# Slots of a routed expert: one plain transfer per expert on SyncE instead of one indirect gather per block on GpSimd, and token gathers one block further ahead

## The chip, the core and the metric

The kernel runs on one core of a Trainium2 chip. The metric is device time in microseconds (us) of one execution. A core has TensorE (PE; its weight loads are PEld), VectorE (DVE), ScalarE (ACT), GpSimd (POOL) and SyncE (SP), each with an instruction queue of its own that is worked off in order, and 16 DMA engines that all queues share. SP issues plain transfers; POOL issues the indirect ones, whose row numbers lie in on-chip memory.

## What is computed

One decoder layer for 1024 tokens of width 1024. The first two thirds (attention and a recurrent mixer) are not touched here. The last third is a mixture of experts: every token is routed to 6 of 64 experts, each a SwiGLU of inner width 256, and a shared expert sees all tokens.

```python
dest = pad_start[sorted_e] + arange(n_assign) - grp_start[sorted_e]   # a slot for each (token, choice)
row_tok[dest], row_w[dest] = token, weight
...
y = swiglu(h[tok], w_gate[e], w_up[e], w_down[e]) * w[:, None]        # per block of slots
out = segment_sum(ys, row_tok)  + swiglu(h, sw_gate, sw_up, sw_down)
```

All arithmetic is float32, done as three products of a high and a low part (`three`), so each expert's weights (three arrays of 1 MB) are split into high and low on ACT and DVE before TensorE can use them.

## The kernel before

**The slot table.** In DRAM, `d_slot` holds 64 x 1152 rows of two words, (token number, weight). While tokens are routed, POOL scatters 48 batches of such rows into it (`route`, line 1676). `ranks` then sorts the experts by how many tokens they got: `eid` (line 1772) holds the expert number of each rank, and `sidx` (line 1779) for each rank and block the table rows of its 128 slots.

**Blocks.** `BLOCKS` gives each rank one to four blocks of at most 128 slots: 84 blocks for 64 experts. `order` mixes experts with several blocks among those with one. In `experts`, blocks 0 to 7 are the shared expert's (their tokens are plain loads), blocks 8 to 91 the routed ones.

**One routed block** needs, in this order: its slots (`slots`, line 1932, an indirect gather of 8 bytes a row by POOL into tile `sl`); its token rows (`rows`, line 1940, an indirect gather by POOL of up to 128 rows of 4 KB into one of four tiles `xg`, with the token numbers in `sl`); a transposition on TensorE (`turn`, lines 1952 and 1965, `tp<-idf,xg`); gate and up products; an activation; the down product; a scaling by weight and gate on DVE (`result`, line 2026, `ye`, three tiles); and an indirect scatter by POOL that adds `ye` onto the rows of `d_acc` in DRAM (line 2028). Scatters add to the same tensor, so each waits until the one before it has landed.

**Order of issue.** In iteration b of the loop in `experts`, the instructions of several blocks are interleaved: the gate/up products of block b, `need_x(b + 3)` (token rows of block b+3), `need_s(b + 5)` (slots of block b+5), the transposition of block b+1, the down product and `result` of block b-1 with its scatter. So POOL's queue reads: scatter of b-2, token rows of b+3, slots of b+5, scatter of b-1, and so on. The first slots, of blocks 8 to 12, are fetched in `dispatch`, and `experts` waits for its mark ("slots", 0) at b = 6, where it asks for the token rows of blocks 8 and 9.

**Weights.** SP issues the three 1 MB loads of an expert (`fetch`, line 1884) after it has read the expert's number out of `eid` into a register (`values_load`). `need_w(k + 4)`, once per expert, brings gate and up of expert k+4 and down of expert k+3; each has three buffers, so SP waits there until the split of an earlier expert is done. In `dispatch`, before the first slots, `need_w` runs for experts 1 to 3: eight loads.

The whole program is interleaved by a planner from the costs that the functions yield (`[("POOL", 1.0)]` and the like); it sets the order in each queue, not when an instruction runs.

Of the kernel before, what the change touches and what calls it, by code (L numbers as in the profile page):

```python
# [8 lines left out]
F32 = mybir.dt.float32  # L9
# [28 lines left out]
class Kern:  # L38
# [1699 lines left out]
    def ranks(self, pg):  # L1738

        nc, i64, t = self.nc, self.i64, self.dt  # L1740
        ps = lambda: pg.tile([128, 512], F32, name="g")
        G = ("alloc", ("g", 2)), ("free", "g")
        cr = ps()
        for j in range(8):
            nc.tensor.matmul(cr[:, 0:NE], self.onesb, self.Mb[:, j, :], start=(j == 0), stop=(j == 7))
        crow = t("crow", [128, NE])
        nc.vector.tensor_copy(crow, cr[:, 0:NE])
        yield [G[0], ("PE", .4), ("DVE", .12), G[1]]
        cc = ps()
        for j in range(8):  # L1750
            nc.tensor.matmul(cc[0:NE, 0:1], self.Mb[:, j, :], self.onesb[:, 0:1], start=(j == 0), stop=(j == 7))
        pk = self.pk = t("pk", [NE, 2])
        nc.vector.tensor_copy(pk[:, 1:2], cc[0:NE, 0:1])
        nc.vector.tensor_copy(pk[:, 0:1], self.tok[0:NE, 0:1])
        yield [G[0], ("PE", .4), ("DVE", .14), G[1]]
        lt = t("lt", [NE, NE])
        nc.vector.tensor_scalar(lt, i64[0:NE], pk[:, 0:1], None, op0=OP.is_lt)
        a = t("a", [NE, NE])
        nc.vector.scalar_tensor_tensor(a, crow[0:NE], pk[:, 1:2], lt, op0=OP.is_equal, op1=OP.mult)
        nc.vector.scalar_tensor_tensor(a, crow[0:NE], pk[:, 1:2], a, op0=OP.is_gt, op1=OP.add)  # L1760
        yield [("DVE*", .45)]
        rank = t("rank", [NE, 1])
        nc.vector.tensor_reduce(rank, a, op=OP.add, axis=AX.X)
        perm = self.perm = t("perm", [NE, NE])
        nc.vector.tensor_scalar(perm, i64[0:NE], rank, None, op0=OP.is_equal)

        eb = t("eb", [NE, 128])
        nc.vector.tensor_copy(eb, pk[:, 0:1].to_broadcast([NE, 128]))
        yield [("DVE*", .4)]
        po = ps()  # L1770
        nc.tensor.matmul(po[:, 0:NE], eb, perm, start=True, stop=True)
        self.eid = t("eid", [1, NE], I32)
        nc.vector.tensor_copy(self.eid, po[0:1, 0:NE])

        self.sidx = []
        for j in range(4):
            n = max(r + 1 for r in range(NE) if len(self.BLOCKS[r]) > j)
            x = t(f"sidx{j}", [128, n], I32)
            nc.vector.tensor_scalar(x, po[:, 0:n], float(SLOTS), self.tok[:, j:j + 1], op0=OP.mult, op1=OP.add)
            self.sidx.append(x)  # L1780
        yield [G[0], ("PE", .2), ("DVE", .5), G[1]]

    def leftover(self, pg):

# [58 lines left out]
    def phase_b(self, pg, close_a4, h2):  # L1843
# [84 lines left out]
            yield [("set", ("shared w", 0))]  # L1928

        def slots(idx, n):  # L1930
            sl = B["fp"].tile([128, 2], F32, name="sl", bufs=8)
            nc.gpsimd.indirect_dma_start(out=sl[0:n], out_offset=None, in_=self.d_slot, in_offset=ind(idx[0:n]))  # L1932
            return sl

        def tokens(sl, n):
            return sl.bitcast(I32)[0:n, 0:1]

        def rows(ti, n):
            x = B["fp"].tile([128, D], F32, name="xg", bufs=4)
            nc.gpsimd.indirect_dma_start(out=x[0:n], out_offset=None, in_=self.d_h2, in_offset=ind(ti), bounds_check=T - 1,  # L1940
                                         oob_is_err=False)
            return x
# [104 lines left out]
                if 0 < kk < NK:  # L2047
                    to[kk] = fetch(self.eid[0:1, order[kk]:order[kk] + 1], which)

        def need_s(b):  # L2050
            if b < NB:
                k, j, n = blocks[b]
                r = order[k]
                sls[b] = slots(self.sidx[j][:, r:r + 1], n) if r >= 0 else None

        def need_t(b):
            if b < NB:
                tis[b] = tokens(sls[b], blocks[b][2]) if sls[b] else self.toki[:, b:b + 1]

        def need_x(b):  # L2060
            if b < NB:
                k, j, n = blocks[b]
                if k == 0:
                    x = xs[b] = B["fp"].tile([128, D], F32, name="xg", bufs=4)
                    nc.sync.dma_start(x, self.d_ht[j])
                else:
                    xs[b] = rows(tis[b], n)

        def weight_of(b):
# [7 lines left out]
        def dispatch():  # L2077
            yield [("wait", ("route", 7))]
            expert_pools()
            yield from self.ranks(pg)  # L2080
            for k in range(1, 4):
                need_w(k)
            yield from self.leftover(pg)
            yield [("wait", ("block pools", 0))]
            for b in range(8, 13):
                need_s(b)
                yield [("POOL", 1.0)]
            yield [("DMA", 4.0)]
            yield [("set", ("slots", 0))]

        def experts():

            yield [("wait", ("block pools", 0))]
            yield [("wait", ("shared w", 0))]
            for b in range(8):
                i = blocks[b][1]
                sls[b], tis[b] = None, self.toki[:, i:i + 1]
            xs[0] = h2[6]
            for b in (1, 2):
                need_x(b)  # L2100
            G = ("alloc", ("g", 2)), ("free", "g")
            xt = turn(xs[0], 128)
            yield [("PE", .9), ("ACT", 1.0), ("~DVE", 1.2)]
            act = None
            for b in range(NB + 1):
                if b < NB:
                    k, j, n = blocks[b]
                    m = max(n, MIN_M)
                    two = xt[1] is None
                    for s in up(xt, sets[k % 2], m):  # L2110
                        if b < 8:
                            yield s
                    z = B["z"]
                    if b < 5:
                        yield [("wait", ("T", blocks[b + 3][1]))]
                        need_x(b + 3)
                    elif b == 6:
                        yield [("wait", ("slots", 0))]
                        for i in range(8, 12):
                            need_t(i)  # L2120
                        need_x(8)
                        need_x(9)
                    elif b > 6:
                        need_x(b + 3)
                    if b > 7:
                        need_s(b + 5)
                    turnover = k + 1 < NK + 1 and (blocks[b - 1][0] != k if k else b == 6)
                    if turnover and k + 1 < NK:
                        work.append(split_gu(raws[k + 1], k + 1))
                    pieces(3)  # L2130
                    if turnover and b < 8:
                        yield [("~ACT", 1.7), ("~DVE*", 1.8)]
                if b < NB and two:
                    low(z)
                if act is not None:
                    at = act_t(*act)
                    if b < 8:
                        yield [G[0], ("PE", .25), ("ACT", .3), ("DVE", .35), G[1]]
                if b + 1 < NB:
                    xt = turn(xs[b + 1], blocks[b + 1][2], b < 7)  # L2140
                    if b < 8:
                        yield [("~ACT", 1.0), ("~DVE*", 1.2)]
                if b < NB and two:
                    join(z)
                if act is not None:
                    for s in down(at, act[1]):
                        if b < 8:
                            yield s
                    zs = B["zs"]
                if b < NB:  # L2150
                    act = swiglu(z, m), m
                    pieces(99)
                    if b < 8:
                        yield [("~ACT", .6), ("~DVE", .35)]
                if b > 0:
                    result(zs, blocks[b - 1][2], weight_of(b - 1), tis[b - 1])
                    if b < 8:
                        yield [("~DVE", 1.35), ("~POOL", 1.0)]
                if b < NB:
                    if k and blocks[b - 1][0] != k:  # L2160
                        work.append(split_d(rawd[k]))
                        pieces(99)
                    if b > 7:
                        need_t(b + 4)
                    if turnover:
                        need_w(k + 4)
                    if turnover and b < 8:
                        yield [("~ACT", 2.0), ("~DVE", 2.3), ("~POOL", 1.0)]
# [93 lines left out]
```

## Time and profile before

| | us |
|---|---|
| median of 3 runs | 2097.12 |
| lowest, highest | 2080.12, 2115.2 |
| the profiled execution | 2093.02 |
| its span, first to last instruction | 2091.1 |

All durations below come from the profiled execution. In its span PE is busy 1858.6 us (89%), DVE 1470.3 (70%), ACT 933.1 (45%), POOL 859.6 (41%); the mean granted TensorE clock is 0.918. The routed experts run from about 1200 us to 2060 us. In a row of the profile, `out<-in` names the tiles by the program's names, `x8` counts merged instructions, a time in square brackets is how long the engine was idle before the instruction, with what ended the idle time ("issue": nothing that the profile shows).

### The profile page before, as it was taken

The page shows a single profiled execution, that of the slowest core. Times are in us where ns is not written, and L with a number is a line of the kernel's source. Part 1 is how long each engine was busy: PE and PEld are TensorE (multiplying, and loading weights), DVE is VectorE, ACT ScalarE, POOL GpSimd, SP SyncE. Part 2 cuts the span into 40 slices and gives each one's busy share as a digit, 9 for nine tenths or more (in the row PEclk, how much of TensorE's full clock was granted, in tenths as well). Part 3 has the DMA queues.
Part 4 walks back from the last instruction along what each step waited for, and adds up shares of the span by engine and source line. Part 5 has one row for each costly group of instructions (what it writes and reads, how often), then busy time and mean ns, then how long its engine had stood idle before and what let it go on. Part 6 is the DMA issues. An engine that isn't in the chain of part 4 may idle for free. (4 is left out here: it accounts for less than half of the span.)

```text
span 2091.1 us, 28436 instructions
## 1 busy us (share of the span) xinstructions
PE 1858.6 (89%) x9729; PEld 1399.2 (67%) x9729; DVE 1470.3 (70%) x2561; ACT 933.1 (45%) x1431; POOL 859.6 (41%) x660
## 2 busy tenths in 40 slices
PE   3999999969997997997999799989988989989993
PEld 3777677747876664654787687767756767766771
DVE  7736867939457555656677758878767878878894
ACT  5443433312322332344323236556545656666673
POOL 1201110100012232335455634765656767766662
PEclk7999789969987888998999899999989999999997
DMA  7125345462756648964664589989889999988874
GB/s 270 36 81 126 88 111 129 131 156 71 216 148 183 190 123 237 133 195 137 229 211 147 159 277 322 314 256 318 293 261 309 304 305 307 326 297 297 307 242 174
DMA packets 268579, 440.03 MB, mean 210 GB/s; under 512 B 127445, under 2 KB 197161, under 8 KB 242450
## 3 DMA queue, kind: packets, MB, share of 16 engines
q1 hardware_dynamic: 210978, 365.47, 54.0%
q0 software_dynamic: 26176, 58.91, 12.4%
q10 hardware_dynamic: 31280, 13.83, 2.5%
q8 instruction: 78, 1.28, 0.3%
q14 instruction: 67, 0.55, 0.1%
HBM read 355.27 MB, written 94.90 MB: 215 GB/s over the span
## 5 line engine op out<-in xcount | busy, mean ns | idle before, releaser
L2028 POOL DMA_INDIRECT d_acc<-ye,sl x84 | 192.1, 2287 | 253.4 <-issue 56.2
L1932 POOL DMA_INDIRECT sl<-d_slot,d_sidx x84 | 201.6, 2400 | 27.5 <-issue 24.7
L1904 ACT ACTIVATE wdh<-down 128x1024 fp32r<-128x1024 f32 x128 | 128.7, 1053 | 82.2 <-PE yd L1976 82.2
L1898 DVE TENSOR_TENSOR gul<-up,guh 128x1024 fp32r<-128x1024 f32 x128 | 155.5, 1215 | 10.4 <-ACT guh L1897 9.7
L1940 POOL DMA_INDIRECT xg<-d_h,sl x84 | 149.0, 1774 | 25.6 <-issue 20.7
L1898 DVE TENSOR_TENSOR gul<-gate,guh 128x1024 fp32r<-128x1024 f32 x128 | 155.2, 1213 | 1.7 <-ACT guh L1897 1.7
L1905 DVE TENSOR_TENSOR wdl<-down,wdh 128x1024 fp32r<-128x1024 f32 x128 | 150.1, 1210 | 0.8
L2026 DVE SCALAR_TENSOR_TENSOR ye<-yd,sl,g 128x512 f32<-128x512 f32 (+12 forms) x168 | 120.2, 740 | 32.0 <-PE yd L1976 32.0
L1897 ACT ACTIVATE guh<-gate 128x1024 fp32r<-128x1024 f32 x128 | 134.1, 1047 | 18.8 <-DMA gate<-in_exp_w_gate_dram 18.8
L1976 PE MATMUL yd<-wdh,ah 128*128 128x512 f32 (+6 forms) x368 | 130.5, 438 | 8.5 <-ACT ah L2012 6.7
L1897 ACT ACTIVATE guh<-up 128x1024 fp32r<-128x1024 f32 x128 | 135.1, 1055 | 1.5 <-DMA up<-in_exp_w_up_dram 1.5
L450 PE MATMUL zp<-hTh,whi 128*128 128x512 f32 x480 | 132.4, 414 | 1.4 <-ACT whi L373 1.4
L450 PE MATMUL zp<-hTl,whi 128*128 128x512 f32 x480 | 132.1, 412 | 0.0
L450 PE MATMUL zp<-hTh,wlo 128*128 128x512 f32 x480 | 131.9, 413 | 0.0
L1976 PE MATMUL gu<-guh,xh 128*128 128x512 f32 (+6 forms) x504 | 127.3, 394 | 0.8 <-ACT xh L1959 0.5
L1976 PE MATMUL gu<-guh,xl 128*128 128x512 f32 (+6 forms) x504 | 127.4, 395 | 0.1
L1976 PE MATMUL yd<-wdh,al 128*128 128x512 f32 (+6 forms) x368 | 123.4, 418 | 4.2 <-DVE al L2014 3.7
L1976 PE MATMUL gu<-gul,xh 128*128 128x512 f32 (+6 forms) x504 | 127.0, 394 | 0.0
L1976 PE MATMUL yd<-wdl,ah 128*128 128x512 f32 (+6 forms) x368 | 122.3, 415 | 0.3 <-DVE wdl L1905 0.3
L2012 ACT ACTIVATE ah<-g 128x256 fp32r<-128x256 f32 (+5 forms) x92 | 31.2, 339 | 179.0 <-PE g L2010 178.3
L450 PEld LDWEIGHTS zp<-hTh,whi 128*128 128x128 f32 x480 | 92.6, 198 | 26.4 <-issue 5.5
L1976 PEld LDWEIGHTS gu<-guh,xh 128*128 128x128 f32 (+6 forms) x504 | 89.1, 177 | 29.1 <-ACT xh L1959 1.0
(477 smaller groups left out, 4238.9 us busy)
## 6 DMA issues: line engine op xcount, KB each, us to landing
gate<-in_exp_w_gate_dram SPq DMA_DIRECT2D x64, 1024.0 KB
up<-in_exp_w_up_dram SPq DMA_DIRECT2D x64, 1024.0 KB
down<-in_exp_w_down_dram SPq DMA_DIRECT2D x64, 1024.0 KB
mw<-in_ada_w_dram SPq DMA_DIRECT2D x32, 512.0 KB
wraw<-in_w_in_dram SPq DMA_DIRECT2D x30, 512.0 KB
xw<-in_ada_w_dram SPq DMA_DIRECT2D x8, 1024.0 KB
xw<-in_x_dram SPq DMA_DIRECT2D x8, 512.0 KB
fb<-d_fb SPq DMA_DIRECT2D x16, 256.0 KB
```

The lines of the kernel that those rows point to most:

```text
L450: nc.tensor.matmul(z, a[:, d, :], b[:, d, hs], start=(n == 0 and d == 0), stop=(n == 2 and d == 7))
L1897: nc.scalar.activation(gh[:, qs, n, :], t[:, qs], AF.Copy)
L1898: nc.vector.tensor_sub(gl[:, qs, n, :], t[:, qs], gh[:, qs, n, :].bitcast(F32))
L1904: nc.scalar.activation(dh[:, j], raw[0][:, j], AF.Copy)
L1905: nc.vector.tensor_sub(dl[:, j], raw[0][:, j], dh[:, j].bitcast(F32))
L1932: nc.gpsimd.indirect_dma_start(out=sl[0:n], out_offset=None, in_=self.d_slot, in_offset=ind(idx[0:n]))
L1940: nc.gpsimd.indirect_dma_start(out=x[0:n], out_offset=None, in_=self.d_h2, in_offset=ind(ti), bounds_check=T - 1, oob_is_err=False)
L1976: nc.tensor.matmul(z, x[:, d, :], w[:, d, cs], start=(m == 0), stop=(m == 3 * n - 1))
L2012: nc.scalar.activation(ah[:, :, 0:n], tp[:, :, 0:n], AF.Copy)
L2026: nc.vector.scalar_tensor_tensor(y[0:n, hs], zs[h][0:n], wt, B["g2"][0:n, hs], op0=OP.mult, op1=OP.mult)
L2028: nc.gpsimd.indirect_dma_start(out=self.d_acc, out_offset=ind(ti), in_=y[0:n], in_offset=None, bounds_check=T - 1, oob_is_err=False, compu ...
```

## The change

Slots are no longer gathered per block by POOL. `need_s(k)` works per expert: SP reads the expert's number once more and issues one plain transfer of the expert's first 128, 256, 384 or 512 table rows into a tile `sk` (nine buffers), from which each block takes its two columns. It is called for experts 1 to 5 in `dispatch`, after the eight weight loads, and then for expert k+6 just ahead of `need_w(k + 4)`. `sidx` goes. Token rows are asked for as `need_x(b + 4)` in place of `need_x(b + 3)`; at b = 6 for blocks 8 and 9 as before, at b = 7 for blocks 10 and 11. The number of `xg` tiles stays at four.

```diff
@@ ranks
-        self.sidx = []
-        for j in range(4):
-            ...
-            nc.vector.tensor_scalar(x, po[:, 0:n], float(SLOTS), self.tok[:, j:j + 1], op0=OP.mult, op1=OP.add)
@@ phase_b
-        def need_s(b):
-            if b < NB:
-                k, j, n = blocks[b]
-                r = order[k]
-                sls[b] = slots(self.sidx[j][:, r:r + 1], n) if r >= 0 else None
+        table = self.d_slot.rearrange("(e r) w -> e r w", e=NE)
+        def need_s(k):
+            if 0 < k < NK:
+                r, nb = order[k], len(self.BLOCKS[order[k]])
+                e = nc.values_load(self.eid[0:1, r:r + 1], engines=(SP,), min_val=0, max_val=NE - 1)
+                sl = B["fp"].tile([128, 4, 2], F32, name="sk", bufs=9)
+                nc.sync.dma_start(sl[:, 0:nb], table[ds(e, 1)].rearrange("e r w -> (e r) w").rearrange(
+                    "(j p) w -> p j w", p=128)[:, 0:nb])
+                for b in range(NB):
+                    if blocks[b][0] == k:
+                        sls[b] = sl[:, blocks[b][1]]
@@ dispatch
-            for b in range(8, 13):
-                need_s(b)
-                yield [("POOL", 1.0)]
+            for k in range(1, 6):
+                need_s(k)
@@ experts
                     elif b == 6:
                         yield [("wait", ("slots", 0))]
-                        for i in range(8, 12):
-                            need_t(i)
-                        need_x(8)
-                        need_x(9)
+                        for i in range(8, 10):
+                            need_x(i)
                     elif b > 6:
-                        need_x(b + 3)
-                    if b > 7:
-                        need_s(b + 5)
+                        if b == 7:
+                            need_x(10)
+                        need_x(b + 4)
...
                     if turnover:
+                        need_s(k + 6)
                         need_w(k + 4)
```

## Rows read from the trace of the kernel before

**Rows 1.** Windows: start:end length, busy us (instructions) of PE, PEld, DVE, ACT, POOL; clock, DMA share, GB/s.
```profile
1200.00:2060.00 860.00, 802.25 (x3715) 610.02 (x3713) 687.96 (x892) 508.72 (x748) 539.90 (x248) 0.96 0.88 289
1500.00:1550.00 50.00, 40.09 (x178) 30.34 (x177) 32.48 (x43) 24.11 (x36) 29.61 (x14) 0.86 0.83 254
1550.00:1600.00 50.00, 50.00 (x239) 36.97 (x238) 45.19 (x58) 34.06 (x48) 35.05 (x13) 1.00 0.98 326
```

**Rows 2.** Token tiles: who waited until what (us, times), 1200 to 2080 us.
```profile
  DMA xg<-d_h,sl: 45.5, 13
...
DMA to landing us min/median/max: 4.3/10.0/14.4
```

**Rows 3.** Timeline of TensorE: transpositions of blocks 8 and 9, and a late one.
```profile
1206.05 1.06 PE L1965 MATMUL tp<-idf,xg 128*128 128x128 f32 x8
...
1215.60 1.06 PE L1965 MATMUL tp<-idf,xg 128*128 128x128 f32 x8
...
1531.45 1.68 PE L1965 MATMUL tp<-idf,xg 108*128 108x108 f32 x8 [9.84 <-DMA xg<-d_h,sl]
```

**Rows 4.** Timeline of POOL and of DVE around the longest wait.
```profile
1509.52 7.16 POOL L2028 DMA_INDIRECT d_acc<-ye,sl  x1 [2.15 <-DVE ye L2026]
1516.98 1.52 POOL L1940 DMA_INDIRECT xg<-d_h,sl  x1 [0.30 <-issue]
...
1528.19 1.60 POOL L2028 DMA_INDIRECT d_acc<-ye,sl  x1 [6.24 <-issue]
...
1517.46 1.40 DVE L2026 SCALAR_TENSOR_TENSOR ye<-yd,sl,g 108x512 f32<-108x512 f32 x2
```

**Rows 5.** Line 2028 (scatters): durations ns, first and last start; landing; 1195 to 2080.
```profile
L2028 POOL DMA_INDIRECT d_acc<-ye,sl x84: 1362/1608/7284, 1236.7 to 2059.3; - x84
L2028 POOL DMA_INDIRECT d_acc<-ye,toki x3: 1597/1614/1917, 1201.6 to 1225.0; - x3
...
DMA to landing us min/median/max: 4.0/8.8/17.8
```

**Rows 6.** Timeline of POOL: scatters held by POOL's queue, first and last of 18.
```profile
1324.05 1.43 POOL L2028 DMA_INDIRECT d_acc<-ye,sl  x1 [0.31 <-DVE xl L1968]
...
2020.54 1.40 POOL L2028 DMA_INDIRECT d_acc<-ye,sl  x1 [0.30 <-issue]
```

**Rows 7.** Line 1932 (slot gathers): durations ns min/median/max, first and last start.
```profile
L1932 POOL DMA_INDIRECT sl<-d_slot,d_sidx x84: 877/1003/6658, 1186.8 to 2018.5; - x84
```

**Rows 8.** Page, part 5: busy us, mean ns of one, idle before.
```profile
L2028 POOL DMA_INDIRECT d_acc<-ye,sl x84 | 192.1, 2287 | 253.4 <-issue 56.2
L1932 POOL DMA_INDIRECT sl<-d_slot,d_sidx x84 | 201.6, 2400 | 27.5 <-issue 24.7
```

**Rows 9.** Timeline of POOL and DVE: a long slot gather beside subtractions.
```profile
1489.69 6.65 POOL L1932 DMA_INDIRECT sl<-d_slot,d_sidx  x1 [0.31 <-issue]
...
1489.71 2.34 DVE L1905 TENSOR_TENSOR wdl<-down,wdh 128x1024 fp32r<-128x1024 f32 x2
...
1494.25 1.21 DVE L1898 TENSOR_TENSOR gul<-gate,guh 128x1024 fp32r<-128x1024 f32 x1
```

**Rows 10.** Timeline of SP: first and last of the first eight weight loads.
```profile
1184.28 0.37 SPq L1884 DMA_DIRECT2D gate<-in_exp_w_gate_dram  x1
...
1190.63 0.34 SPq L1884 DMA_DIRECT2D down<-in_exp_w_down_dram  x1
```

**Rows 11.** Timeline of POOL: the first gather of token rows.
```profile
1193.64 1.02 POOL L1940 DMA_INDIRECT xg<-d_h,sl  x1 [0.30 <-DMA sl<-d_slot,d_sidx]
```

**Rows 12.** Timeline of ACT: first uses of the first two weight loads.
```profile
1190.20 1.06 ACT L1897 ACTIVATE guh<-gate 128x1024 fp32r<-128x1024 f32 x1 [18.80 <-DMA gate<-in_exp_w_gate_dram]
1192.76 1.06 ACT L1897 ACTIVATE guh<-up 128x1024 fp32r<-128x1024 f32 x1 [1.51 <-DMA up<-in_exp_w_up_dram]
```

**Rows 13.** DMA queue of small packets: packets, MB, share of 16 engines; from the page.
```profile
q10 hardware_dynamic: 31280, 13.83, 2.5%
```

**Rows 14.** Waits of SP's queue, 1200 to 2080 us: total us, times, longest.
```profile
SPq L1884 <- DVE gul L1898: 388.1, 76, 27.7
```

More of the change, by code (lines that the diff above doesn't have):

```diff
@@ L1773, in ranks @@
         nc.vector.tensor_copy(self.eid, po[0:1, 0:NE])
-        self.sidx = []
-        for j in range(4):
-            n = max(r + 1 for r in range(NE) if len(self.BLOCKS[r]) > j)
-            x = t(f"sidx{j}", [128, n], I32)
-            nc.vector.tensor_scalar(x, po[:, 0:n], float(SLOTS), self.tok[:, j:j + 1], op0=OP.mult, op1=OP.add)
-            self.sidx.append(x)
-        yield [G[0], ("PE", .2), ("DVE", .5), G[1]]
+        yield [G[0], ("PE", .2), ("DVE", .1), G[1]]
     def leftover(self, pg):
@@ L1930, in slots @@
         def slots(idx, n):
-            sl = B["fp"].tile([128, 2], F32, name="sl", bufs=8)
+            sl = B["fp"].tile([128, 2], F32, name="sl", bufs=2)
             nc.gpsimd.indirect_dma_start(out=sl[0:n], out_offset=None, in_=self.d_slot, in_offset=ind(idx[0:n]))
@@ L2048, in need_w @@
                     to[kk] = fetch(self.eid[0:1, order[kk]:order[kk] + 1], which)
-        def need_s(b):
-            if b < NB:
-                k, j, n = blocks[b]
-                r = order[k]
-                sls[b] = slots(self.sidx[j][:, r:r + 1], n) if r >= 0 else None
+        table = self.d_slot.rearrange("(e r) w -> e r w", e=NE)
[9 more added lines that the diff above has]
+                        sls[b] = sl[:, blocks[b][1]]
         def need_t(b):
             if b < NB:
-                tis[b] = tokens(sls[b], blocks[b][2]) if sls[b] else self.toki[:, b:b + 1]
+                tis[b] = tokens(sls[b], blocks[b][2])
         def need_x(b):
@@ L2066, in need_x @@
                 else:
+                    need_t(b)
                     xs[b] = rows(tis[b], n)
@@ L2162, in experts @@
                         pieces(99)
-                    if b > 7:
-                        need_t(b + 4)
                     if turnover:
+                        need_s(k + 6)
                         need_w(k + 4)
```

## The prediction, made before the changed kernel was run

> **What bounds the kernel now.** I read the windows first. In the stage of the routed experts, 1200 to 2060 us, TensorE is busy 802 of 860 us [rows 1]; in 1550 to 1600 it has no gap at all, in 1500 to 1550 it idles 9.91 us and its granted clock falls to 0.86. So TensorE sets the pace and has holes. The token tiles name the holes: transpositions waited 13 times, 45.5 us in all, until a gather of token rows landed [rows 2]; the longest wait is 9.84 us [rows 3].
>
> A hole also costs clock. The window with the long wait holds 178 matmuls, the one after it 239: 61 fewer, at 50/239 = 0.209 us each 12.8 us of work lost for 9.91 us idle. At that ratio the 45.5 us cost 45.5 x 12.8/9.91 = 59 us. That is the most that earlier token rows can give.
>
> Why are the rows late? I followed one case through POOL's queue. The gather that TensorE waited for at 1531 was issued at 1516.98, behind a scatter that began at 1509.52 and lasted 7.16 us [rows 4]. The scatter after it began at 1528.19, although its `ye` had been ready since 1517.46 + 1.40 = 1518.86, and although POOL had been idle for 6.24 us before it. What it waited for was the landing of the scatter before: scatters go one at a time. 87 of them begin between 1201.6 and 2059.3 [rows 5], one per 857.7/86 = 9.97 us, and the median time to landing is 8.8 us of that. TensorE on its own would need (857.7 - 59)/86 = 9.29 us per block; a full block takes it 1215.60 - 1206.05 = 9.55 [rows 3]. **So POOL's chain of scatters is about as slow as TensorE**, and token rows, which stand behind a scatter in the same queue, are late whenever this chain has fallen a block behind.
>
> **The change, part by part.**
>
> *One block more of lead.* `need_x(b + 4)` stands where `need_x(b + 3)` stood, behind the same scatter, and is needed one block later: 9.55 us more. The tile it overwrites is that of block b, transposed an iteration earlier, so four tiles suffice. If the scatters were fast and only now and then late, this would cover nearly each wait (longest 9.84). But their chain runs at 9.97 per block with 9.29 wanted, so its lag grows until TensorE waits again; the lead delays this once. Gain: one block, 9.5 us; bounds 0 (lag refilled at once) and 59 (rival A).
>
> *84 slot gathers leave POOL.* 201.6 us of POOL's time, 2.40 us mean and 1.00 median [rows 7, 8]. Most lies in the wait for a landing and costs nothing. It counts where a scatter began directly, about 0.30 us, behind other work of POOL: 18 of them [rows 6]. Each begins at best one ordinary gather earlier, 1.00 + 0.30 = 1.3 us: 18 x 1.3 = 23 us at most. Half of it I expect to reach TensorE, which doesn't wait in every stretch: 11.5 us.
>
> Why only 1.3 us, where many slot gathers last 6.6? One began at 1489.69 and ended at 1496.34, 0.9 us after DVE's run of subtractions of the weights' low parts, 1489.71 to 1495.46 [rows 9]: POOL stood still while they ran. Without this gather the next instruction of POOL that falls into such a run stands still instead. The Trainium skill (SBUF — State Buffer, section "SBUF: two separate sides") says that DVE with two inputs in SBUF holds a port pair that GpSimd's operations need, and that the loser blocks fully; the trace agrees, with 6.65 us against the 1.00 median. By that rule a transfer issued by SyncE escapes the block, but not the gathers and scatters that stay on POOL.
>
> *The first slots move behind the first weights.* This part costs. Slots of block 8 were gathered by POOL at once, and its token rows were asked for at 1193.64 [rows 11]; TensorE transposed them at 1206.05. Now the slots of experts 1 to 5 are SP's next transfers after eight loads of 1 MB issued from 1184.28 to 1190.63 [rows 10]. That queue hands over one load after the other: the first two, the head of these eight, were first used at 1190.20 and 1192.76 by ACT, which had waited for each [rows 12], so 2.56 us per MB. The eighth lands at 1190.20 + 7 x 2.56 = 1208.1 at the earliest, and at 1190.20 + 7 x 3.63 = 1215.6 at the stage's mean of 289 GB/s [rows 1]. Fewer gathers compete early on, so I take 1209.5. The token rows follow 0.3 us later, and land 4.3 to 14.4, median 10.0, us after issue [rows 2]: at 1219.8. TensorE stops for 1219.8 - 1206.05 = 14 us; with 2 us of lowered clock behind it (2.9 behind the 9.91 above), 16 us, that nothing hides, since block 8 is TensorE's next work. Bounds: 1208.1 + 0.3 + 4.3 gives 6.6; 1215.6 + 0.3 + 10.0 gives 19.9, with clock 22.8. Zero, if small transfers overtake the loads.
>
> The Trainium skill (DMA: Bandwidth & Descriptors, "Queues, rings and completion order") says that an SP queue's descriptors are consumed in ring order, while different queues take turns. By that rule the slots wait for all eight loads, whereas POOL's queue took turns with them. [rows 12] agree as far as equal loads go; a small transfer behind a large one isn't in these rows.
>
> *Later slots.* Per expert SP reads one register more and issues one transfer more. Eight loads with their register reads took 1190.63 - 1184.28 = 6.35 us [rows 10], so about 0.8 us per expert of 13.4 us. SP spends 388 us waiting for DVE's splits [rows 14], and weights have three buffers: nothing. If that cover were gone, 63 x 0.8 = 50 us. Slots of expert k+6 leave two experts, 27 us, before the token rows need them; three loads of 3.63 us ahead of them make 11. SP might wait for a free `sk` tile, but nine are more than the blocks in flight.
>
> *DMA.* 84 x 128 = 10752 rows of 8 bytes replace 7616 (the block sizes' sum). The queue of small packets prices one at 2.5% of 16 engines' 2091 us over 31280 [rows 13], 27 ns: 3136 more cost 3136 x 0.027/16 = 5 us of each engine, in a stage with a share of 0.88 [rows 1]. I take 0 and keep 5 for the top of the range. The four small DVE operations of `sidx` leave: below 0.5 us together by their width against [rows 9].
>
> **Sum**: -9.5 - 11.5 + 16 = -5, from the profiled execution's 2093.0 (span 2091.1 and 1.9 around it; 4.1 below the median of 2097.1): **2088 us**. This case's own range: 2093 - 9.5 - 23 + 6.6 = 2067 to 2093 + 22.8 + 5 = 2121.
>
> **Rivals.** *A, all waits go.* The waits were single late gathers, and one block of lead (9.55) covers each. 2093 - 59 + 16 = 2050, without the stop at the start 2034. For it: no wait is longer than 9.84, and the gather's median landing is 10.0. Against: scatters at 9.97 per block, which no extra lead makes faster. Chance 0.17.
>
> *B, slower: the block by DVE moves onto the scatters.* Slot gathers absorbed 84 x (2.40 - 1.00) = 118 us of standing still. If scatters, each of which delays the next, now take half, that is 59 us in the chain: 2093 - 5 + 59 = 2147. It decides once a scatter's mean duration goes from 2.29 us [rows 8] beyond about 2.29 + 47/84 = 2.85, which makes +42. Against: a scatter that now begins inside a run of subtractions mostly stood behind a slot gather held by the same run. Chance 0.08.
>
> *C, the start costs nothing*, small transfers overtake the loads: 2093 - 21 = 2072, inside my range and its chance.
>
> **How the numbers follow.** The forecast with C has 0.75, A 0.17, B 0.08. 2% of the median is 42 us, about what a measurement of this kernel, whose runs spread over 35 us, can tell from no change: faster means below 2055, slower above 2139. So A is faster, B slower, the rest within. The range 2046 to 2122 holds this case and A with its stop; A without it and B lie outside.
>
> **What would show it.** Right: a wait of 7 to 20 us ahead of TensorE's first routed transposition; later waits for token rows fewer, but not gone (15 to 35 us in all); scatters still spaced about 9.6 to 9.9 us with a median landing near 8.8. Wrong: no waits left after the start (A), a scatter's mean duration near 3 us (B), a first token gather issued before 1200 us after a start like today's (C).

## The result, and the profile after

The change made the kernel slower. The median of four runs is 2161.7 us (2150.12 to 2164.13) against 2098.43 for the kernel before on the same chip (four runs): ratio 1.0306, 95% interval 1.026 to 1.0352. The forecast of 2088 us and its range to 2122 are both below it. All ratios and intervals compare fast executions of the two kernels on the same chip (now and then one is slower), so a ratio can differ by some tenths of a per cent from the quotient of the medians. The profiled execution of the changed kernel took 2164.13 us, span 2162.3, mean granted clock 0.904 (before 0.918).

Of the 71 us between the two spans, 50 lie between the start of block 8's scatter and that of block 91's (822.5 us before, 872.7 after). 14 lie in the new stop at the start. What is left, some 7 us, was there before the routed experts began (the scatter of block 0 starts at 1140.7 in place of 1132.3). Over all the kernels below that start lies between 1127 and 1141, and block 0 comes before anything that the change moves, so I don't count it to the change; where it comes from no run tells.

**The start** is as forecast in place and size. The timeline of the changed kernel, SP, POOL and TensorE (start us, duration us, instruction, idle time before it and what ended it):

```profile
1199.10 0.34 SPq L1877 DMA_DIRECT2D down<-in_exp_w_down_dram  x1
1200.28 13.92 SPq L2051 DMA_DIRECT2D sk<-d_slot  x6
...
1218.75 1.06 POOL L1933 DMA_INDIRECT xg<-d_h,sk  x1 [25.54 <-DMA sk<-d_slot]
...
1228.03 1.33 PE L1958 MATMUL tp<-idf,xg 128*128 128x128 f32 x5 [14.39 <-DMA xg<-d_h,sk]
```

The first slot transfer leaves SP at 1200.28, behind the eighth load (1199.10). POOL gets the slots at 1218.75, 18.5 us later. TensorE stands still for 14.39 us; I had 14. The first token gather had been issued at 1193.64 before [rows 11]. The same slot transfer ahead of the loads is of use after 2.9 us at most (experiment 4), so what it waits for here are the megabytes ahead of it in its queue. That agrees with the ring order of which the Trainium skill tells (DMA: Bandwidth & Descriptors, "Queues, rings and completion order").

**SP** now waits for something that wasn't in the forecast. Waits of SP's queue after, 1200 to 2130 us (total us, times, longest):

```profile
SPq L2051 <- DMA d_acc<-ye,sk: 416.6, 52, 20.7
SPq L1877 <- DVE gul L1891: 126.0, 29, 26.1
```

Before, SP was held by the splits on DVE, 388.1 us [rows 14]. That wait has shrunk to 126.0, and in its place SP waits 52 times, 416.6 us, at the slot transfer, until a scatter has landed.

**POOL, DVE and TensorE**: part 5 of the page after (busy us, mean ns of one, idle us before it with its releaser), the row of `ye` from the page before, then the waits of TensorE after, 1200 to 2150:

```profile
L2021 POOL DMA_INDIRECT d_acc<-ye,sk x84 | 233.3, 2777 | 452.1 <-DVE ye L2019 173.0
L2019 DVE SCALAR_TENSOR_TENSOR ye<-yd,sk,g 128x512 f32<-128x512 f32 (+12 forms) x168 | 119.5, 741 | 138.2 <-issue 61.9
L1933 POOL DMA_INDIRECT xg<-d_h,sk x84 | 179.4, 2135 | 50.9 <-DMA sk<-d_slot 25.5
L1969 PEld LDWEIGHTS yd<-wdh,al 128*128 128x128 f32 (+6 forms) x368 | 63.0, 183 | 94.6 <-DVE al L2007 74.7
```

```profile
L2026 DVE SCALAR_TENSOR_TENSOR ye<-yd,sl,g 128x512 f32<-128x512 f32 (+12 forms) x168 | 120.2, 740 | 32.0 <-PE yd L1976 32.0
```

```profile
PE yd L1969 <- DVE al L2007: 51.5, 32, 3.2
PE tp L1958 <- DMA xg<-d_h,sk: 24.9, 10, 14.4
PE tp L1945 <- DMA xg<-d_h,sk: 11.7, 6, 3.2
```

The scatter's own duration rose from 2287 ns [rows 8] to 2777. Waits for token rows beyond the start fell by half: 24.9 + 11.7 less the 14.4 of the start are 22.2 us, against 45.5 [rows 2]. But DVE idles 138.2 us ahead of `ye` (32.0 before), and TensorE has a wait that it hardly had: 51.5 us (3.7 before) for `al`, the low part of the activations, which DVE makes.

**How these hang together** shows in one stretch after, SP, DVE, POOL and TensorE:

```profile
1548.70 0.35 SPq L2051 DMA_DIRECT2D sk<-d_slot  x1
1549.90 0.34 SPq L1877 DMA_DIRECT2D gate<-in_exp_w_gate_dram  x1
1550.48 0.33 SPq L1877 DMA_DIRECT2D up<-in_exp_w_up_dram  x1
1551.63 0.34 SPq L1877 DMA_DIRECT2D down<-in_exp_w_down_dram  x1
1561.64 0.34 SPq L2051 DMA_DIRECT2D sk<-d_slot  x1
...
1548.77 1.41 DVE L2019 SCALAR_TENSOR_TENSOR ye<-yd,sk,g 128x512 f32<-128x512 f32 x2 [9.20 <-issue]
1550.09 1.22 DVE L1891 TENSOR_TENSOR gul<-gate,guh 128x1024 fp32r<-128x1024 f32 x1
...
1553.49 0.30 DVE L2007 TENSOR_TENSOR al<-g,ah 128x144 fp32r<-128x144 f32 x1
...
1561.62 1.40 DVE L2019 SCALAR_TENSOR_TENSOR ye<-yd,sk,g 56x512 f32<-56x512 f32 x2 [5.44 <-DMA d_acc<-ye,sk]
...
1549.55 1.61 POOL L2021 DMA_INDIRECT d_acc<-ye,sk  x1 [8.86 <-DVE ye L2019]
1551.47 1.86 POOL L1933 DMA_INDIRECT xg<-d_h,sk  x1 [0.30 <-issue]
1562.39 2.08 POOL L2021 DMA_INDIRECT d_acc<-ye,sk  x1 [9.06 <-DVE ye L2019]
...
1553.85 1.13 PE L1969 MATMUL yd<-wdh,al 128*72 128x512 f32 x2 [1.64 <-DVE al L2007]
```

At 1561.62 a landing lets DVE write the next `ye`; at 1561.64 SP's slot transfer goes out, at 1562.39 the next scatter starts. 1548.70, 1548.77 and 1549.55 are the same three steps one block earlier (the profile names no releaser for that `ye`, but the scatter before had landed at 1548.69). All three engines wait for the same scatter. What SP and DVE then start falls on the next one. SP sends the slots and an expert's three megabytes within 2.93 us (1548.70 to 1551.63), just as the scatter starts; it lands 10.4 us after its end, against 6.71 on average. DVE, having made `ye`, runs its overdue subtractions beside the scatter and the gather behind it. This scatter still took 1.61 us only; others, as at 1521.70 with 7.79 us, last until such a run is over. `al` comes behind the subtractions at 1553.49, and TensorE stops for it.

Before, such loads went out one by one, most of them behind a split. SP's timeline before:

```profile
1505.27 0.34 SPq L1884 DMA_DIRECT2D gate<-in_exp_w_gate_dram  x1
1508.22 0.33 SPq L1884 DMA_DIRECT2D up<-in_exp_w_up_dram  x1
1511.81 0.34 SPq L1884 DMA_DIRECT2D down<-in_exp_w_down_dram  x1
1515.21 0.34 SPq L1884 DMA_DIRECT2D gate<-in_exp_w_gate_dram  x1
```

No weights came too late for it: ACT waited for `gate` and `up` once each in the whole execution after, 18.9 and 1.4 us, much as at the start before [rows 12]. If SP's wait costs time, it is by when the loads run.

### The profile page after: what moved, and what is told of

Its sections match the earlier page's. It is cut to its first block, busy times and chain, and to the rows that moved or that the text cites. A ratio compares the mean times of both kernels' runs of the same rounds, so it can differ in the third digit from the quotient of the medians.

```text
span 2162.3 us, 28802 instructions
## 1 busy us (share of the span) xinstructions
PE 1887.6 (87%) x9729; PEld 1412.5 (65%) x9729; DVE 1464.9 (68%) x2557; ACT 932.1 (43%) x1431; POOL 732.1 (34%) x576
## 3 DMA queue, kind: packets, MB, share of 16 engines
q8 instruction: 78, 1.28, 0.2%
## 5 line engine op out<-in xcount | busy, mean ns | idle before, releaser
L2021 POOL DMA_INDIRECT d_acc<-ye,sk x84 | 233.3, 2777 | 452.1 <-DVE ye L2019 173.0
L2019 DVE SCALAR_TENSOR_TENSOR ye<-yd,sk,g 128x512 f32<-128x512 f32 (+12 forms) x168 | 119.5, 741 | 138.2 <-issue 61.9
L1933 POOL DMA_INDIRECT xg<-d_h,sk x84 | 179.4, 2135 | 50.9 <-DMA sk<-d_slot 25.5
L1969 PE MATMUL yd<-wdh,al 128*128 128x512 f32 (+6 forms) x368 | 132.9, 446 | 52.4 <-DVE al L2007 51.5
L1890 ACT ACTIVATE guh<-gate 128x1024 fp32r<-128x1024 f32 x128 | 134.1, 1048 | 18.9 <-DMA gate<-in_exp_w_gate_dram 18.9
L1969 PE MATMUL yd<-wdl,ah 128*128 128x512 f32 (+6 forms) x368 | 127.4, 427 | 3.9 <-DVE wdl L1898 3.9
L1969 PEld LDWEIGHTS yd<-wdh,al 128*128 128x128 f32 (+6 forms) x368 | 63.0, 183 | 94.6 <-DVE al L2007 74.7
```

Source lines behind the costliest of these rows:

```text
L1890: nc.scalar.activation(gh[:, qs, n, :], t[:, qs], AF.Copy)
L1969: nc.tensor.matmul(z, x[:, d, :], w[:, d, cs], start=(m == 0), stop=(m == 3 * n - 1))
L2019: nc.vector.scalar_tensor_tensor(y[0:n, hs], zs[h][0:n], wt, B["g2"][0:n, hs], op0=OP.mult, op1=OP.mult)
L2021: nc.gpsimd.indirect_dma_start(out=self.d_acc, out_offset=ind(ti), in_=y[0:n], in_offset=None, bounds_check=T - 1, oob_is_err=False, compu ...
```

## The experiments

Theory: a tile `sk` is free only when the scatter of its expert's last block has landed. The scatters lag so far behind that nine tiles are too few, SP waits, and what it sends late and in a burst slows the scatters. Rivals: the extra block of lead does it alone (three tiles `ye` hold DVE); the stop at the start; the block by DVE that slot gathers used to absorb (rival B); the slot transfers' small packets.

The table says where a block's time goes, worked out from starts, ends and landings of the scatters of blocks 8 to 91 in each profiled execution: the span from the first start to the last, then the means in us of the scatter instruction, of landing after its end, of the pause until the next one starts, and of the lag of a scatter's start behind its finished `ye`.

| kernel | span | instruction | landing | pause | lag |
|---|---|---|---|---|---|
| before | 822.5 | 2.29 | 6.33 | 1.23 | 8.1 |
| after (lead 4, 9 tiles) | 872.7 | 2.78 | 6.71 | 0.96 | 15.7 |
| lead back (lead 3, 9 tiles) | 813.7 | 2.31 | 6.52 | 0.91 | 7.3 |
| lead 4, 16 tiles | 821.0 | 2.49 | 6.42 | 0.92 | 14.1 |
| before with the lead | 842.7 | 2.65 | 6.16 | 1.28 | 16.8 |
| slots first (lead 4, 9 tiles) | 886.0 | 2.81 | 6.87 | 0.92 | 17.8 |
| lead 3, 8 tiles | 868.4 | 2.59 | 6.87 | 0.93 | 10.4 |
| no low parts | 805.7 | 1.51 | 7.25 | 0.89 | 15.5 |
| slots first, 16 tiles, lead 3 | 806.6 | 2.32 | 6.47 | 0.87 | 7.0 |
| slots first, 16 tiles, lead 4 | 833.8 | 2.49 | 6.57 | 0.92 | 14.5 |

From before to after a block takes 0.49 us more of instruction, 0.38 more of landing and 0.27 less of pause: 0.60 us, over 83 intervals the 50 us.

**1. The lead taken back** (against the changed kernel):

```diff
-                        if b == 7:
-                            need_x(10)
-                        need_x(b + 4)
+                        need_x(b + 3)
```

> The changed kernel with token rows asked for three blocks ahead again; the slots still come by SyncE, behind the first weights. Theory 1 (the extra block of lead lets TensorE run ahead until the three ye tiles hold up VectorE, whose subtractions then start together with a scatter and stop it): about 45 us faster than the changed kernel, near 2115, with VectorE's idle time before ye back from 138 to some 30 us and a scatter's mean duration back from 2.78 to about 2.3 us; the stop of 14 us at the start stays. Theory 2 (SyncE waits for scatters to free one of nine slot tiles, so weights go out together with the next scatter and slow its landing): 2140 or more, since nine tiles stay nine. Theory 3 (the small packets on SyncE's queue cost): unchanged, near 2160.

2103.45 us, ratio to before 1.0073 (1.0032 to 1.0114; ten runs). SP's wait is shorter, 158.9 us, and DVE's idle time ahead of `ye` is 29.6, as before the change. Part 5 of its page and SP's waits:

```profile
L2021 POOL DMA_INDIRECT d_acc<-ye,sk x84 | 194.3, 2313 | 466.3 <-DVE gul L1891 131.4
L2019 DVE SCALAR_TENSOR_TENSOR ye<-yd,sk,g 128x512 f32<-128x512 f32 (+12 forms) x168 | 119.9, 739 | 29.6 <-PE yd L1969 29.6
```

```profile
SPq L2051 <- DMA d_acc<-ye,sk: 158.9, 38, 10.8
```

So one block of lead, thought to be a gain, is worth over 2% of loss with nine tiles, though here no slot gather is left on POOL: its scatters last 2313 ns. The leaving of the slot gathers alone does not lengthen the scatters, which speaks against rival B's cause.

**2. Sixteen tiles `sk`**, lead and all else as changed:

```diff
-                sl = B["fp"].tile([128, 4, 2], F32, name="sk", bufs=9)
+                sl = B["fp"].tile([128, 4, 2], F32, name="sk", bufs=16)
```

> The changed kernel with 16 slot tiles in place of nine, so that SyncE need not wait for a scatter's landing. Theory 2: SyncE's 417 us of waiting for scatters goes, weights are paced by the splits again, landing after a scatter's issue goes from 6.7 back to 6.3 us, 2110 to 2125. Theory 1: the wait goes but the time stays within 10 us of 2162. Theory 3: unchanged.

2100.03 us, ratio 1.0064 (1.0021 to 1.0107; ten runs). Its waits of SP's queue:

```profile
SPq L1877 <- DVE gul L1891: 319.4, 74, 26.1
...
SPq L2051 <- DMA d_acc<-ye,sk: 0.4, 1, 0.4
```

One number, the count of a tile of 32 bytes per partition, gives back 2.4 of the 3.1%. SP is again paced by DVE. The slot transfers are the same in number and size, so small packets can explain no more than the 0.64% that are left.

**3. The lead alone**, in the kernel before; slots stay on POOL and come a block earlier too (`sl` has twelve tiles in place of eight for it):

```diff
-                        need_x(b + 3)
+                        need_x(b + 4)
...
-                        need_s(b + 5)
+                        need_s(b + 6)
```

> The kernel before with token rows asked for four blocks ahead and the slots, still gathered by GpSimd per block, six ahead. Theory 1: slower than before by 30 to 50 us (2130 to 2150), with VectorE idle before ye for over 100 us. Theory 2 and theory 3: no loss, 2080 to 2100, as nothing on SyncE changes.

2114.7 us, ratio 1.0107 (1.0027 to 1.0186): a loss, where my sum had a gain of 9.5 us. Part 5 of its page:

```profile
L2028 POOL DMA_INDIRECT d_acc<-ye,sl x84 | 222.4, 2647 | 251.9 <-issue 65.5
L2026 DVE SCALAR_TENSOR_TENSOR ye<-yd,sl,g 128x512 f32<-128x512 f32 (+12 forms) x168 | 118.8, 740 | 114.1 <-DMA d_acc<-ye,sl 54.2
```

Waits for token rows do fall, from 45.5 us to 38.8. But the scatters now lag 16.8 us behind their `ye`, in place of 8.1. With three tiles `ye`, DVE must wait for landings: 114.1 us idle, of which 54.2 are put down to `d_acc`. TensorE waits 22.1 us for `al`, against 3.7 before.

**4. The first slots ahead of the weights**, the rest as changed:

```diff
+            for k in range(1, 6):
+                need_s(k)
...
-            for k in range(1, 6):
-                need_s(k)
```

(The tiles `sk` move to a pool that is open by then; still nine.)

> The changed kernel with the slots of experts 1 to 5 issued by SyncE ahead of the first eight weight loads. All theories: the first wait of TensorE for token rows goes from 14.4 us to under 3, and the time falls by 12 to 18 us, to about 2147. If a chain of scatters alone set the end, less than 8 us would come back.

2150.98 us, ratio 1.0296 (1.0231 to 1.0362), beside 1.0306 for the change: 0.1 ± 0.8%, so the times alone can't tell nothing from the 0.7% that 14 us would be. The stop of 14.39 us is gone (TensorE transposes block 8 without a wait). The first slot transfer and the gather that needs it:

```profile
1188.51 5.00 SPq L2051 DMA_DIRECT2D sk<-d_slot  x5
...
1191.40 1.06 POOL L1933 DMA_INDIRECT xg<-d_h,sk  x1 [3.90 <-PE g L1830]
```

But SP's wait for scatters grows to 490.5 us and TensorE's for `al` to 65.7, and in the profiled executions the first routed scatter starts 12 us earlier (1245.7 against 1257.7), the last one no earlier (2131.7 against 2130.4). Where the scatters set the pace, an earlier start of TensorE is lost again to them.

**5. Eight tiles, lead 3** (experiment 1 with one tile less):

```diff
-                sl = B["fp"].tile([128, 4, 2], F32, name="sk", bufs=9)
+                sl = B["fp"].tile([128, 4, 2], F32, name="sk", bufs=8)
```

> Token rows three blocks ahead as before the change, slots by SyncE, and only eight slot tiles, so that SyncE waits for a scatter one expert younger and its weight loads go out behind a landing. Theory 2 (loads in step with the scatters slow their landing, whatever the lead): SyncE waits over 300 us for scatters, landing from the end of a scatter's instruction takes 6.7 us or more on average, and the time is 20 to 50 us above that with nine tiles and the same lead (2103), so 2125 to 2150. Theory 1 (the lead and the three ye tiles do it): unchanged, 2095 to 2110.

2152.29 us, ratio 1.0264 (1.0177 to 1.0352): one tile less costs 1.9 ± 1.0%, without the extra block of lead. SP's waits, the row of the scatters' landing, and TensorE's waits:

```profile
SPq L2051 <- DMA d_acc<-ye,sk: 513.1, 60, 17.3
```

```profile
DMA to landing us min/median/max: 3.8/9.9/15.0
```

```profile
PE tp L1958 <- DMA xg<-d_h,sk: 82.8, 32, 13.6
```

In experiment 1 that median is 8.6 us and the same wait of TensorE 50.7 us (13 us of each are the stop at the start). DVE is idle ahead of `ye` for 41.2 us only (138.2 in the change), so this loss doesn't need the three tiles `ye`: a late SP is enough.

**6. No subtractions of the weights' low parts.** The change, with the `gul` subtractions of all routed experts but the first and the `wdl` subtractions of all of them left out, so that part of the sum of products is missing:

```diff
+                    if k < 2:
                         nc.vector.tensor_sub(gl[:, qs, n, :], ...)
...
-                nc.vector.tensor_sub(dl[:, j], raw[0][:, j], dh[:, j].bitcast(F32))
```

> The changed kernel without the subtractions that make the low parts of the routed weights (from the third expert on the old low parts are used). If GpSimd stands still while VectorE subtracts two tiles in SBUF, the scatters' mean duration falls from 2.78 to 1.5 to 1.6 us, the token gathers' from 2.14 to 1.0 to 1.1, none lasts over 3 us, and the chain of scatters from block 8 to 91 falls from 873 to under 800 us. If the long instructions come from the DMA queues instead, durations over 4 us stay (15 of 84).

2088.66 us, in a single execution. The rows of lines 1933 (gathers) and 2021 (scatters), durations ns min/median/max, here and then after the change:

```profile
L1933 POOL DMA_INDIRECT xg<-d_h,sk x84: 949/1038/1102, 1212.8 to 2025.8; - x84
...
L2021 POOL DMA_INDIRECT d_acc<-ye,sk x84: 1329/1510/1627, 1249.2 to 2054.9; - x84
```

```profile
L1933 POOL DMA_INDIRECT xg<-d_h,sk x84: 950/1610/6114, 1218.7 to 2097.2; - x84
...
L2021 POOL DMA_INDIRECT d_acc<-ye,sk x84: 1347/1800/7847, 1257.7 to 2130.4; - x84
```

No gather lasts over 1102 ns and no scatter over 1627; after the change the maxima were 6114 and 7847. So everything beyond about 1.1 us of a gather and 1.6 us of a scatter is the block by DVE's subtractions. The prediction read this from one gather [rows 9]. The Trainium skill (SBUF — State Buffer, "SBUF: two separate sides") says there that a DVE instruction with two inputs in SBUF contends with a GpSimd instruction that reads SBUF; all 168 transfers, whose row numbers lie in SBUF, agree. The same section of the Trainium skill also tells of a probe in which `tensor_tensor`, the operation of these subtractions, did not stall a DMA; these transfers it does hold up. The scatters' span falls to 805.7 us only, since landing rises to 7.25: SP still waits 411.1 us.

**7. The slots' move without its costs**: lead 3, 16 tiles, first slots ahead of the weights (edits 1, 2 and 4 together).

> The part of the change that moves the slots to SyncE, freed of its two side costs: 16 slot tiles, first slots ahead of the first weights, token rows three blocks ahead as before. Theory 1 and 2: no stop at the start, no waiting of SyncE for scatters, so 10 to 25 us faster than the kernel before, 2065 to 2085. Theory 3 (small packets on SyncE's queue cost): no faster than before.

2084.54 us, ratio 0.9964 (0.9932 to 0.9996; ten runs). SP never waits for `sk`; none of the scatters is held by POOL's queue, where 18 were [rows 6]. TensorE's waits for token rows are 35.4 us (45.5 before).

**8. Two sums.** The kernel before, with the scatters of even and odd blocks added to two tensors that are joined at the end, so that a scatter needn't wait for the one before it:

```diff
-            nc.gpsimd.indirect_dma_start(out=self.d_acc, ...
+            nc.gpsimd.indirect_dma_start(out=self.d_acc2 if odd else self.d_acc, ...
...
+                nc.sync.dma_start(y, self.d_acc2[i * 128:(i + 1) * 128, :])
+                nc.vector.tensor_add(x, x, y)
```

> The kernel before with the scatters of even and odd blocks going to two tensors that are added at the end, so that a scatter waits for the one before the last. If the chain of scatters is what makes token rows late, the waits for token rows (45.5 us) fall under 10 us and the time falls by 30 to 55 us less some 10 to 15 us for the longer end: 2045 to 2075. If the rows are late for another reason, the waits stay and the time rises by the longer end, to about 2105.

2058.49 us, ratio 0.9833 (0.9754 to 0.9912; six runs). TensorE's waits for token rows nearly vanish:

```profile
PE tp L1967 <- DMA xg<-d_h,sl: 2.6, 4, 0.9
...
PE tp L1954 <- DMA xg<-d_h,sl: 1.2, 2, 0.9
```

45.5 us became 3.8. No transfer is faster (the scatters' landing has a median of 10.6 us, against 8.8 [rows 5]); only their order is loosened. So the chain of scatters was what made token rows late.

**9. Lead 4 with 16 tiles and the first slots first** (experiment 7 with the lead).

> The changed kernel with both side costs off: 16 slot tiles and the first slots ahead of the first weights; token rows four blocks ahead. It differs from the run with three blocks of lead (0.9964 of the kernel before) in the lead alone. Theory 1: the lead costs 10 to 25 us there too (0.3 to 1.2% slower than that run), with VectorE held up before ye for over 70 us. Theory 2 alone: no difference, or a gain of some 10 us as the prediction had it.

2100.54 us, ratio 0.9996 (0.9962 to 1.0029; ten runs). Against experiment 7 the lead costs 0.32 ± 0.46%, so that it gives no gain of 0.45% (9.5 us) is shown, that it costs time here is not. What theory 1 expected of DVE is there: 85.8 us idle ahead of `ye` (26.5 in experiment 7). SP waits 0.2 us for `sk`.

**10 and 11. Two sums with the slots' move**, at lead 3 and lead 4 (experiment 8's edit on kernels 7 and 9).

> Two sums, slots by SyncE with 16 tiles and ahead of the first weights, three blocks of lead. If the chain of scatters was the last thing that made GpSimd matter, the time is within 10 us of two sums with GpSimd's slot gathers (0.983 of the kernel before, some 2058). If GpSimd's queue still held scatters up there (58 of 84 began directly behind other work of GpSimd), 5 to 20 us faster, 2040 to 2055.

> The same with four blocks of lead. With the chain halved, scatters stay close behind ye, so the lead neither helps nor hurts: within 8 us of the run with three blocks. If the lead costs by itself (tiles, queue order), slower by 15 us or more.

2055.82 us, ratio 0.9768 (0.9696 to 0.984), and 2053.46 us, ratio 0.9746 (0.9675 to 0.9818): both faster than the kernel before and kernels 7 and 9, the same within their intervals, and not clearly apart from experiment 8. TensorE's waits for token rows are 0.4 us in all in the first and none in the second. Part 5 of the page of the second:

```profile
L2023 POOL DMA_INDIRECT d_acc<-ye,sk x84 | 396.8, 4723 | 231.6 <-DVE ye L2021 207.8
```

A scatter lasts 4723 ns here, and the kernel is none the slower: the next scatter no longer waits for its landing. Why it is so much longer than the 2746 ns of experiment 8 shows in its timeline, POOL's row and then DVE's:

```profile
1504.93 6.85 POOL L2023 DMA_INDIRECT d_acc<-ye,sk  x1 [0.73 <-DMA sk<-d_slot]
...
1504.54 2.34 DVE L1900 TENSOR_TENSOR wdl<-down,wdh 128x1024 fp32r<-128x1024 f32 x2
...
1509.08 1.21 DVE L1893 TENSOR_TENSOR gul<-gate,guh 128x1024 fp32r<-128x1024 f32 x1
```

A scatter that waits for nothing but its `ye` starts 0.3 us behind it on average (3.6 in experiment 8), just where DVE goes on with its subtractions, and stands still with them: this one ends 1.5 us after the run, at 1511.78. 59 of the 84 scatters last over 2.5 us, and each of these ends 1.2 to 1.5 us after such a run.

## Why the prediction was wrong

**The difference in steps.** Call the kernel of experiment 7 kernel 7, and so on. Kernels 7, 9, 2 and the change differ by one thing each (that the tiles `sk` lie in another pool in 7 and 9 changes no work). In percent of the kernel before, the half-widths of two intervals joined as the root of their squares' sum:

| step | measured | us of 2097 | predicted us |
|---|---|---|---|
| slots leave POOL (before to 7) | -0.36 ± 0.32 | -8 | -11.5 |
| one block more of lead (7 to 9) | +0.32 ± 0.46 | +7 | -9.5 |
| first slots behind the weights (9 to 2) | +0.68 ± 0.54 | +14 | +16 |
| nine tiles in place of 16 (2 to the change) | +2.42 ± 0.63 | +51 | 0 |

That the sum, 64 us, is the measured difference (2161.70 - 2098.43 = 63) is no proof, as each step starts where the one before ends. What the table shows is how the difference divides in this order.

**The step that failed** is the last: "Later slots. [...] SP might wait for a free `sk` tile, but nine are more than the blocks in flight." I counted blocks between gather and scatter, and tiles belong to experts: the transfer for expert k+6 takes the tile of expert k-3, and its last reader is not a computation but the scatter of that expert's last block, until it has landed. With scatters 15.7 us behind their `ye` this is late, and the transfer stands ahead of the next weights in SP's queue. In place of nothing it cost 2.42 ± 0.63%, 51 us, with 416.6 us of waiting for `sk` in SP's queue. I had named what SP was waiting for ("388 us waiting for DVE's splits [rows 14]") and taken it as slack; it was what spaced the loads. The loss of that cover I had priced at 50 us by SP's own instructions, and left out of the range; that this is the size found is chance, for the way is another.

How a late SP costs time: three pairs of kernels differ only in the tiles.

| pair | SP's wait for `sk`, us | instruction | landing | ratio |
|---|---|---|---|---|
| 16 to 9, lead 4 (2 to the change) | 0.4 to 416.6 | +0.29 | +0.29 | 1.0064 to 1.0306 |
| 9 to 8, lead 3 (1 to 5) | 158.9 to 513.1 | +0.28 | +0.35 | 1.0073 to 1.0264 |
| 16 to 9, lead 4, slots first (9 to 4) | 0.2 to 490.5 | +0.32 | +0.30 | 0.9996 to 1.0296 |

Each time a scatter's instruction and its landing grow by about 0.3 us each: 83 x 0.6 = 50 us in a chain without slack. That the tile's count does it through scatters that last and land longer is shown. That what a scatter lasts beyond some 1.6 us is DVE's subtractions beside it is shown by experiment 6. That the landing grows because more loads set out close to a scatter is argued: no run spaces the loads while SP waits. Counts in the traces speak for it. After the change, the seven scatters of 128 rows with no weight load issued within 4 us of their start landed 4.8 us after their end on average, the 21 with two or three such loads 8.7 us; with 16 tiles (experiment 2) it is 4.5 us for six and 9.4 us for 21. And in each of the three pairs the mean number of such loads per scatter rises as tiles go: 1.52 to 1.90, 1.81 to 2.08 and 1.60 to 2.01.

**One block of lead** is the second step that failed: a loss or nothing in place of a gain of 9.5 us. "But their chain runs at 9.97 per block with 9.29 wanted, so its lag grows until TensorE waits again" was right in that the lag grows, but I let token rows be what TensorE waits for next. Token rows a block earlier let it run a block further ahead of the scatters, and what is late next is a tile `ye`: DVE stops, works in order, and `al` behind it stops TensorE. In the kernel before this costs 1.07% (experiment 3), with the other costs gone 0.32 ± 0.46%, which may be nothing. With nine tiles it is also what makes SP late: the lead taken back lowers 1.0306 to 1.0073. The two failures feed each other: with lead 3, nine tiles and the late start together cost 1.09 ± 0.52% (kernels 7 to 1), with lead 4 the nine tiles alone 2.42%. So their prices can't be had by undoing one alone; each undoing gives back some 2.4%. That three tiles `ye` are what holds DVE is not tested by a run with more of them.

**The start** was right in place and size, 14.39 us against 14, and not by luck: the eighth load left SP 8.5 us later than before, and with that the slots were forecast for 1218.0 and came at 1218.75. Its worth is 0.68 ± 0.54% with 16 tiles. With nine, 0.1 ± 0.8%, the times leave it open; there the chain of scatters ended no earlier without the stop.

**Slots off POOL**: right in sign and mechanism, 18 held scatters became 0 in kernels 1 and 7 (seven are left with lead 4, in kernel 9 and the change, behind token gathers), and near in size, -8 ± 7 against -11.5 us.

**The bound** was right, and the forecast didn't follow from it what it should have. "POOL's chain of scatters is about as slow as TensorE" is shown by experiments 8, 10 and 11: with the order loosened and hardly a wait for token rows left, the 84 scatters spread over 770.6, 766.4 and 766.8 us, 9.23 to 9.28 us per block, where the prediction gave TensorE on its own 9.29. (The one late gather that it followed [rows 4] was no pure case: it stood behind a scatter of 7.16 us, but also took some 14.4 us to land, the longest of all [rows 2].) Any delay of a scatter is then paid in full; I looked for what the change takes off the chain and not for all that now hangs on a landing: SP, by the tiles `sk`, and DVE, by the tiles `ye`.

**The rivals.** A (all waits go) fell: even without side costs (kernel 9) 37.9 us of waits for token rows stay. B named the right symptom, longer scatters; 2.777 us is short of its 2.85, and its cause is not the missing slot gathers (2.31 us without them in kernels 1 and 7) but DVE and SP, both released by the landing for which POOL waits too. C fell with the 14.39 us. Of the signs that I had named, the stop and the later waits for token rows (22.2 us, in 15 to 35) came, these last in part by luck, as TensorE waits for `al` instead; the scatters' spacing (10.51 us, not 9.6 to 9.9) and median landing (9.8, not 8.8) did not. My expectations missed as well: experiments 1 to 3 came out faster than expected (the lead alone cost about half of what I had), experiment 4 gave back 0.1 ± 0.8% where 0.6 to 0.9 were expected, and in experiment 6 the chain stayed above 800 us.

## What to carry to other kernels

Before a tile moves to another queue, look up its last reader: when that is a transfer, the tile comes free at a landing, and a queue that works in order makes everything behind it wait for that landing. A wait that an engine has in plenty is not always slack; it may be what spaces its transfers. And where a chain of transfers is as slow as the bound engine, more lead moved the wait to the next tile with few buffers; loosening the chain itself (two sums, -1.7% alone, -2.3 and -2.5% with the slots moved) was worth more than moving the slots alone (-0.4%).

## What the runs showed of the hardware beyond that

Without DVE's subtractions of two tiles of SBUF, 168 indirect transfers of POOL all took 0.95 to 1.63 us (experiment 6); beside them, up to 7.85. A slot transfer that left SP 1.2 us behind the last of eight loads of 1 MB was of use 18.5 us later; ahead of them, 2.9 us later at most (experiment 4). And scatters that add to different tensors can be in flight together at no loss: in kernel 11 the next one starts 3.4 us before the one before has landed, on average, and the kernel is 2.5% faster than before, though an instruction there lasts 4.72 us.
